# A two-block network: a convolution without GpSimd, and a state space preparation with own work tiles, lagged matmuls and loads one tile ahead

## The chip, the cores and the metric

The kernel runs on one core of one Trainium2 chip. The metric is the device time of one execution in microseconds, from the first to the last instruction of the program.

## The reference, cut to what matters

Two blocks run one after the other on 256 latent tokens and 256 context tokens of width 1024. The first block has four half-weight feed-forward layers, a convolution module and a neighbourhood attention. The second has four feed-forward layers, an attention mixer and a state space mixer (S5). The change touches the convolution, and the preparation of the state space tables from the weights alone.

```python
CONV_WIDTH = 31
def _conv_module(h, w1, b1, wdw, bdw, lng, lnb, w2, b2):
    a, gt = jnp.split(h @ w1 + b1, 2, axis=-1)
    u = a * jax.nn.sigmoid(gt)
    u = lax.conv_general_dilated(u, wdw[:, None, :], ..., feature_group_count=u.shape[-1]) + bdw
    u = jax.nn.silu(_layernorm(u, lng, lnb))
    return u @ w2 + b2
...
def s5_discretise(lam_re, lam_im, b_re, b_im, log_step):
    dt = jnp.exp(log_step)[:, None]
    mag = jnp.exp(lam_re * dt)
    a_re, a_im = mag * jnp.cos(lam_im * dt), mag * jnp.sin(lam_im * dt)
    ...
    bb_re = f_re[..., None] * b_re - f_im[..., None] * b_im
    bb_im = f_re[..., None] * b_im + f_im[..., None] * b_re
    return a_re, a_im, bb_re, bb_im
# s5_scan: x_t = a * x_{t-1} + bb u_t ;  y_t = Re(c x_t), in both directions
```

The kernel runs the scan in blocks of eight steps. For that it needs, for each of eight tiles of state groups, the powers of `a`, the inputs `a^k bb` (table V), the outputs `a^k c` (table O), the products of the two (a Toeplitz block, K and T) and rotations over the blocks (table E). None of these depends on the tokens.

## The kernel before, in words

**Matmuls in three passes.** A float32 weight piece of 128x1024 is loaded into `raw`, rounded to `wh` by ScalarE (L180), and the rest `wl = raw - wh` is formed by VectorE or GpSimd (L185). Each product is then three matmuls (`gemm`, L212). Which engine forms `wl` is set by `self.cvm`: 0 gives all to VectorE, 2 gives every second one to GpSimd (L183). Feed-forward layers over both streams set it to 0 and set it back to 2 at their end, so the convolution before the change runs with 2.

**Order.** The program is written as one stream of matmuls. `mm` (L105) adds each matmul's estimated cost to a clock `pe_t`, and `tick` then steps background tasks whose time has come. A `Task` is a generator. After each `yield` it waits for its period of `pe_t`, or for the number that was yielded if that is more, and at least half a period. The tile framework then places the instructions of each engine by its own estimate of when they are ready, so the order on an engine can differ from the written one. Every engine runs its queue strictly in the resulting order. All DMAs are issued by SyncE (SP), also in order.

**Stages.** In the order of time: the feed-forward layer f100, the convolution, the layers f102 and f110, then attention and the rest. During the three feed-forward layers two tasks run beside the matmuls: the modulation vectors (`mods`, `jk` on VectorE, L535) and the preparation `s5_pre` with a period of 820.

**The convolution** (`conv`, L947) works on eight tiles of 128 channels, both streams side by side (128x512). For each tile: 48 matmuls `pj` (`pw1`), a gate `u` on VectorE (L969), then 31 taps. Eight taps go to GpSimd: ScalarE scales a shifted `u` into `pr` (L998) and GpSimd adds it to `a` (L999). Five go to TensorE as matmuls `ptap` with diagonal weights `dgw` (L1018). The other 18 go to VectorE, ScalarE making the first; two running sums `v` and `b` (L986, L1004) are added in L1007, then `a` (L1021), then the matmul's result (L1022). The matmuls of tile m's taps and its last additions (`rest`) come after the 48 matmuls of tile m+1, and the sums `pmean` for the layer norm (L1029) one tile later still. The last tile runs the streams apart, with 12 taps on TensorE, 7 on GpSimd and 12 on VectorE. Then the layer norm starts with eight subtractions (L1057).

**The preparation** (`s5_pre`, L1853) loops over eight tiles d. In each it loads B and C (`bc`, one buffer, L1955), forms powers `pn`, `pw` on VectorE, with the work tiles `pt` that the rotations use on GpSimd, then `bb` on GpSimd (L1947 to L1952), copies `bb` to `bbz` on ScalarE (L2003, L2004), and for both directions r: six GpSimd products for V (L2015 to L2025), eight transposes `pvt` on TensorE, copies back by ScalarE (L2033) into the same work tiles `w`, their store to `dV`, six GpSimd products for O in the tiles `w` again (L2041 to L2051), their store to `dO`, and eight matmuls `kp`. Then follow the rotations `E` on GpSimd (L2079 to L2098), also in tiles `w`, and the Toeplitz loads and stores (L1967, L1969).

## Time and profile before

| what | value |
|---|---|
| time, median of three runs | 3753.76 us |
| lowest and highest of the three | 3747.49 and 3756.62 us |
| the profiled execution | 3753.8 us |
| its span, first to last instruction | 3752.0 us |
| mean granted TensorE clock | 0.963 of full speed |
| TensorE matmul, VectorE, ScalarE, GpSimd busy | 93%, 71%, 38%, 32% |

The profile is one execution. A page and several views of its trace were read: the busy share of each engine in stretches of time, groups of instructions by line and shape with the idle time of the engine just before them and what ended it, who waited for whom, and the instructions of a stretch in order of time. PE is TensorE, DVE is VectorE, ACT is ScalarE, POOL is GpSimd and SP is SyncE. A full TensorE clock is written 1.00; half is 0.5.

### The profile page before, as it was taken

Reading aid. Unit: us, or ns where it says so; the run is one execution under the profiler, and the core shown is the slowest. Engines: PE = TensorE matmul, PEld = TensorE weight load, DVE = VectorE, ACT = ScalarE, POOL = GpSimd, SP = SyncE. Lnnn points to the kernel's source line nnn. Section 1 sums busy time; section 2 is a strip of 40 time slices with the busy share of each in tenths; the row PEclk is TensorE's granted clock in tenths of the full one; section 3 lists DMA queues with packets and bytes.
Section 4 is the critical chain, followed back from the end, with each engine's and each line's share of the span. In section 5 each row is a group of like instructions: output and inputs, shape, how many; then the busy total and the mean of one; then the engine's idle time right before and its main releaser. Section 6 shows DMA issues by size and latency. Waiting matters only on the chain. (4 is left out here: it accounts for less than half of the span.)

```text
span 3752.0 us, 54881 instructions
## 1 busy us (share of the span) xinstructions
PE 3495.2 (93%) x21110; PEld 3055.5 (81%) x21110; DVE 2652.6 (71%) x4326; ACT 1424.2 (38%) x2500; POOL 1218.5 (32%) x1057
## 2 busy tenths in 40 slices
PE   8989977999999899998999998999999999997898
PEld 7767855988898687898998888778888988885798
DVE  7988699776669786777987775786665633368633
ACT  4222344532233223555343223565322432243443
POOL 5545366244445355213430003333000300035343
PEclk9999988999999999999999999999999999998899
DMA  7565310254546863424655542103555332238353
GB/s 258 184 207 194 118 57 34 102 192 164 167 146 211 293 211 130 144 89 160 244 217 199 185 165 96 62 29 107 180 192 178 135 124 92 100 114 281 113 191 125
DMA packets 158127, 580.42 MB, mean 155 GB/s; under 512 B 25252, under 2 KB 56740, under 8 KB 118184
## 3 DMA queue, kind: packets, MB, share of 16 engines
q1 hardware_dynamic: 157864, 576.91, 44.4%
q8 instruction: 166, 2.72, 0.3%
q14 instruction: 97, 0.79, 0.1%
HBM read 547.55 MB, written 29.29 MB: 154 GB/s over the span
## 5 line engine op out<-in xcount | busy, mean ns | idle before, releaser
L180 ACT ACTIVATE wh<-raw 128x1024 fp32r<-128x1024 f32 (+1 forms) x679 | 701.2, 1038 | 1268.4 <-PE gu L106 728.5
L106 PE MATMUL gu<-hl,wh 128*128 128x512 f32 (+1 forms) x3136 | 1084.6, 347 | 5.4 <-DVE hl L693 4.4
L106 PE MATMUL gu<-hh,wh 128*128 128x512 f32 (+1 forms) x3136 | 1078.9, 348 | 8.4 <-ACT hh L690 7.8
L106 PE MATMUL gu<-hh,wl 128*128 128x512 f32 (+1 forms) x3136 | 1083.2, 347 | 2.8 <-DVE wl L185 2.5
L185 DVE TENSOR_TENSOR wl<-raw,wh 128x1024 fp32r<-128x1024 f32 (+1 forms) x537 | 694.1, 1295 | 401.2 <-ACT wh L180 389.8
L185 POOL TENSOR_TENSOR wl<-raw,wh 128x1024 fp32r<-128x1024 f32 (+1 forms) x142 | 360.1, 2537 | 1259.4 <-ACT wh L180 1214.7
L535 DVE CUSTOM_DVE_ANT_0 jk<-mw,cb,vec 128x1024 bf16<-128x1024 f32 x480 | 705.8, 1470 | 29.7 <-DMA mw<-in_mw_dram 19.0
L106 PEld LDWEIGHTS gu<-hl,wh 128*128 128x128 f32 x3136 | 600.5, 192 | 79.1 <-DVE hl L693 6.1
L106 PEld LDWEIGHTS gu<-hh,wh 128*128 128x128 f32 x3136 | 597.0, 192 | 81.7 <-ACT hh L690 9.4
L106 PEld LDWEIGHTS gu<-hh,wl 128*128 128x128 f32 x3136 | 600.2, 192 | 74.3 <-DVE wl L185 3.5
L106 PE MATMUL pd<-Hh,wh 128*128 128x256 f32 (+1 forms) x1696 | 562.7, 334 | 27.4 <-ACT Hh L779 27.3
L106 PE MATMUL pd<-Hl,wh 128*128 128x256 f32 (+1 forms) x1696 | 563.6, 334 | 1.6 <-DVE Hl L780 1.5
L106 PE MATMUL pd<-Hh,wl 128*128 128x256 f32 (+1 forms) x1696 | 563.5, 334 | 0.0
L106 PEld LDWEIGHTS pd<-Hh,wh 128*128 128x128 f32 x1696 | 323.9, 192 | 60.3 <-ACT Hh L779 29.3
L106 PEld LDWEIGHTS pd<-Hl,wh 128*128 128x128 f32 x1696 | 324.5, 192 | 33.5 <-DVE Hl L780 2.8
L106 PEld LDWEIGHTS pd<-Hh,wl 128*128 128x128 f32 x1696 | 324.5, 192 | 30.3 <-issue 0.2
L777 DVE TENSOR_TENSOR gu<-sg,gu 128x512 f32<-128x512 f32 (+1 forms) x196 | 113.2, 578 | 205.5 <-PE gu L106 196.0
L106 PE MATMUL pj<-hh,wh 128*128 128x256 f32 (+1 forms) x736 | 230.4, 330 | 16.9 <-ACT hh L690 6.9
L106 PE MATMUL pj<-hh,wl 128*128 128x256 f32 (+1 forms) x736 | 232.3, 320 | 0.9 <-DVE wl L185 0.9
L106 PE MATMUL pj<-hl,wh 128*128 128x256 f32 (+1 forms) x736 | 231.1, 319 | 1.7 <-DVE hl L1086 1.0
L779 ACT ACTIVATE Hh<-gu 128x512 fp32r<-128x512 f32 (+1 forms) x196 | 98.7, 503 | 287.6 <-DVE gu L777 287.6
L106 PEld LDWEIGHTS pj<-hh,wh 128*128 128x128 f32 x736 | 145.5, 206 | 28.9 <-ACT hh L690 8.2
(407 smaller groups left out, 4656.3 us busy)
## 6 DMA issues: line engine op xcount, KB each, us to landing
raw<-in_gu_dram SPq DMA_DIRECT2D x186, 1024.0 KB, 4.8
mw<-in_mw_dram SPq DMA_DIRECT2D x280, 512.0 KB, 4.2
raw<-in_dn2b_dram SPq DMA_DIRECT2D x38, 1024.0 KB, 4.7
raw<-in_dn1b_dram SPq DMA_DIRECT2D x32, 1024.0 KB, 6.2
raw<-in_dn1a_dram SPq DMA_DIRECT2D x16, 768.0 KB, 4.3
raw<-in_pw_dram SPq DMA_DIRECT2D x12, 1024.0 KB, 4.7
raw<-in_dn2a_dram SPq DMA_DIRECT2D x16, 768.0 KB, 4.2
dV<-w SPq DMA_DIRECT2D x32, 256.0 KB, 4.2
```

Source lines behind the costliest of these rows:

```text
L106: ins = self.last_mm = self.nc.tensor.matmul(out=out, lhsT=lhsT, rhs=rhs, start=start, stop=stop, **kw)
L180: ins = nc.scalar.activation(out=h2, in_=r, func=AF.Copy)
L185: self.low_p = lambda eng=eng, l2=l2, r=r, h2=h2: eng.tensor_sub(l2, r, h2.bitcast(F32))
L535: self.behind_pe(nc.vector.tensor_tensor_reduce(out=jk, in0=tl[i], in1=self.cb[s], scale=1.0, scalar=self.V(f"mod_b{b}{l}")[:, j:j + 1], o ...
L777: nc.vector.tensor_mul(pr[:, :n], sg[:, :n], pu[:, :n])
L779: nc.scalar.activation(out=hi, in_=pr[:, :n], func=AF.Copy)
```

## The change

In the convolution GpSimd gets no taps. TensorE takes 8 instead of 5 (14 instead of 12 on the last tile), and VectorE and ScalarE the remaining 23, of which ScalarE makes the first of each running sum, so VectorE has 21 instead of 16 scaled additions. The addition of `a` (L1021) and the scaled copies for it (L987, L998) are gone. All `wl` of the convolution go to VectorE (`cvm = 0`).

In the preparation the period becomes 1500. `bc` and `pw` get two buffers, and `bc` of tile d+1 is loaded at the start of tile d. VectorE's powers use their own work tiles `pq`. The V products have tiles `vw`, the O products `ow` and the transposed V `vt`. The copies to `bbz` move from ScalarE to GpSimd. The steps stand in another order: V and O products of direction 1, then the transposes of V; V of direction 0, then the `kp` matmuls of direction 1; and so on, so that each matmul is written some steps after the product that it reads.

```diff
-    def conv(self, ready, gate, after, NPE=5, NPOOL=8, L=1, n1_=12, n2_=7):
+    def conv(self, ready, gate, after, NPE=8, L=1, n_last=14):
...
-                pk, ek, dk = range(n_pool), range(n_pool, n_pool + n_pe), list(range(n_pool + n_pe, W))
+                ek, dk = range(n_pe), list(range(n_pe, W))
...
-                first = [nc.vector.tensor_scalar(b2, src(dk[1]), w(dk[1]), None, ALU.mult)]
-                nc.scalar.activation(out=a2, in_=src(0), func=AF.Copy, scale=w(0))
+                nc.scalar.activation(out=b2, in_=src(dk[1]), func=AF.Copy, scale=w(dk[1]))
+                first = []
...
-                for k in pk[1:]:
-                    diagonal()
-                    pr = cp.tile([128, 2, T], F32, tag="pr", name="pr", bufs=2)[:, :ns]
-                    nc.scalar.activation(out=pr, in_=src(k), func=AF.Copy, scale=w(k))
-                    nc.gpsimd.tensor_add(a2, a2, pr)
...
-                    nc.vector.tensor_add(vm, vm, a2)
                     nc.vector.tensor_add(vm, vm, pe)
...
+            self.cvm = 0
             w0 = [self.take() for _ in range(2)]
...
-            bc = sp.tile([128, 4, 2, 4, 16], F32, tag="bc", name="bc")
+            bc = sp.tile([128, 4, 2, 4, 16], F32, tag="bc", name="bc", bufs=2)
...
+        ahead = load(0)
         for d in range(8):
-            bc = load(d)
+            bc = ahead
+            if d < 7:
+                ahead = load(d + 1)
...
-                a.activation(out=bbz[i][0:64, :, :, 0:16], in_=bb[i][0:64], func=AF.Copy)
-                a.activation(out=bbz[i][64:128, :, :, 16:32], in_=bb[i][64:128], func=AF.Copy)
+                g.tensor_copy(bbz[i][0:64, :, :, 0:16], bb[i][0:64])
+                g.tensor_copy(bbz[i][64:128, :, :, 16:32], bb[i][64:128])
...
-                A, B, C = [sp.tile([128, 4, 9, 16], F32, tag=f"w{i}", name=f"w{i}") for i in range(3)]
+                A, B, C = [sp.tile([128, 4, 8, 16], F32, tag=f"vw{i}", name=f"vw{i}") for i in range(3)]
...
-                    vt = (C8, A8)[i].rearrange("p q e h -> p (q e h)")
+                    vt = sp.tile([128, 512], F32, tag=f"vt{i}", name=f"vt{i}")
...
-                A, B, C = [sp.tile([128, 4, 9, 16], F32, tag=f"w{i}", name=f"w{i}") for i in range(3)]
+                A, B, C = [sp.tile([128, 4, 9, 16], F32, tag=f"ow{i}", name=f"ow{i}") for i in range(3)]
...
+            V1 = yield from inputs(1)
+            O1 = yield from outputs(1)
+            yield from turned(1, V1)
+            V0 = yield from inputs(0, lambda: store_outputs(1, O1))
+            yield from steps(1, O1)
+            O0 = yield from outputs(0)
+            yield from turned(0, V0)
+            E = yield from rotations()
+            store_outputs(0, O0)
+            yield from steps(0, O0)
+            store_rotations(E)
...
-            pre = Task(self, self.s5_pre(sp), 820)
+            pre = Task(self, self.s5_pre(sp), PRE_STEP)
```

`turned` holds the transposes `pvt`, `steps` the matmuls `kp`, `inputs` and `outputs` the six GpSimd products each. The scratch for dynamic DMA descriptors is also cut to 1024, which gives room in the on-chip memory.

How the instructions now stand is shown at three places. The first is VectorE in the convolution, around the end of one tile's taps. `u` is the gated input of a tile, `v` and `b` its running sums, `a` GpSimd's sum. Before:

```order
L969 SCALAR_TENSOR_TENSOR u_3858<-th,t 128x256 x2
L1004 SCALAR_TENSOR_TENSOR v_3869<-u_3857,vec,v_3869 128x512
L1004 SCALAR_TENSOR_TENSOR b_4570<-u_3857,vec,b_4570 128x512
L986 TENSOR_SCALAR b_4703<-u_3858,vec 128x512
L1004 SCALAR_TENSOR_TENSOR v_3870<-u_3858,vec,v_3870 128x512
L1007 TENSOR_TENSOR v_3869<-v_3869,b_4570 128x512
L1004 SCALAR_TENSOR_TENSOR b_4703<-u_3858,vec,b_4703 128x512
...
L1021 TENSOR_TENSOR v_3869<-v_3869,a_4569 128x512
...
L1022 TENSOR_TENSOR v_3869<-v_3869,ptap 128x512
```

And VectorE at the end of a tile's taps in the changed kernel, with its own line and buffer numbers:

```order
L186 TENSOR_TENSOR wl<-raw,wh 128x1024
L995 SCALAR_TENSOR_TENSOR b_4442<-u_3892,vec,b_4442 128x512
...
L998 TENSOR_TENSOR v_3903<-v_3903,b_4319 128x512
L970 SCALAR_TENSOR_TENSOR u_3893<-th,t 128x256 x2
L995 SCALAR_TENSOR_TENSOR v_3904<-u_3892,vec,v_3904 128x512
...
L1012 TENSOR_TENSOR v_3903<-v_3903,ptap 128x512
...
L995 SCALAR_TENSOR_TENSOR v_3905<-u_3893,vec,v_3905 128x512
```

The addition of `a` and the first scaling of `b` are gone from VectorE, and from tile to tile there are two `wl` where there was one; the taps of neighbouring tiles interleave as before.

The second place is ScalarE in f100, at the start of the preparation's second tile. `Hh` and `sg` belong to the feed-forward layer, `wh` to its weights. Before:

```order
L779 ACTIVATE Hh_701<-gu 128x512
L2003 ACTIVATE bbz_1013<-bb_2211 64x8x16
L2004 ACTIVATE bbz_1013<-bb_2211 64x8x16
L180 ACTIVATE wh<-raw 128x1024
L775 ACTIVATE sg<-gu 128x512
L2003 ACTIVATE bbz_1014<-bb_2212 64x8x16
L2004 ACTIVATE bbz_1014<-bb_2212 64x8x16
...
L779 ACTIVATE Hh_702<-gu 128x512
```

ScalarE at the same place in the changed kernel:

```order
L780 ACTIVATE Hh_701<-gu 128x512
L181 ACTIVATE wh<-raw 128x1024
L776 ACTIVATE sg<-gu 128x512
...
L780 ACTIVATE Hh_702<-gu 128x512
L181 ACTIVATE wh<-raw 128x1024 x5
L2037 ACTIVATE vt_2522<-pvt 128x512
```

The four copies to `bbz`, which read what GpSimd makes from the loaded `bc`, no longer stand ahead of the feed-forward layer's own work.

The third place is GpSimd in the first tile of the preparation, at the end of V's products for direction 1. Before:

```order
L2019 TENSOR_TENSOR w_1168<-w_1168,w_1170 128x512
L2023 TENSOR_TENSOR w_1170<-pw_1022,bb_1099 128x512
L2025 TENSOR_TENSOR w_1169<-w_1169,w_1170 128x512
L2047 TENSOR_TENSOR w_1360<-pw_1022,bc 128x576
L2043 TENSOR_TENSOR w_1361<-pw_1022,bc 128x576
L2041 TENSOR_TENSOR w_1359<-pw_1021,bc 128x576
L2045 TENSOR_TENSOR w_1359<-w_1359,w_1361 128x576
```

GpSimd at the same place in the changed kernel:

```order
L2009 TENSOR_TENSOR vw_1327<-pw_1180,bb_1287 128x512
L2017 TENSOR_TENSOR vw_1328<-pw_1180,bb_1288 128x512
L2046 TENSOR_TENSOR ow_1404<-pw_1180,bc 128x576
L2011 TENSOR_TENSOR vw_1329<-pw_1181,bb_1288 128x512
L2048 TENSOR_TENSOR ow_1406<-pw_1181,bc 128x576
L2052 TENSOR_TENSOR ow_1405<-pw_1181,bc 128x576
L2013 TENSOR_TENSOR vw_1327<-vw_1327,vw_1329 128x512
```

Before, the O products write the buffers that the V store still reads; now both kinds have their own tiles and interleave.

## Rows read from the trace of the kernel before

**Rows 1.** The page, part 1: busy us, share of span, instructions of each engine.

```profile
PE 3495.2 (93%) x21110; PEld 3055.5 (81%) x21110; DVE 2652.6 (71%) x4326; ACT 1424.2 (38%) x2500; POOL 1218.5 (32%) x1057
```

**Rows 2.** Stretches: busy us and instructions per engine, clock, DMA share, GB/s.

```profile
250.00:300.00 50.00, 39.34 (x183) 32.01 (x184) 46.67 (x63) 13.32 (x18) 28.10 (x20) 0.86 0.58 191
...
550.00:600.00 50.00, 32.78 (x113) 22.92 (x113) 50.00 (x52) 23.11 (x43) 30.29 (x17) 0.85 0.13 42
...
950.00:1000.00 50.00, 50.00 (x239) 40.99 (x238) 30.84 (x37) 15.46 (x22) 27.07 (x18) 1.00 0.44 150
...
1250.00:1300.00 50.00, 36.57 (x166) 29.13 (x165) 45.26 (x55) 14.23 (x22) 28.37 (x19) 0.88 0.85 299
```

**Rows 3.** DVE groups, 470 to 650 us: count, busy us, mean ns, idle before.

```profile
L1004 DVE SCALAR_TENSOR_TENSOR v<-u,vec,v 128x512 f32<-128x512 f32 x56 | 69.7, 1251 | 0.0
L1004 DVE SCALAR_TENSOR_TENSOR b<-u,vec,b 128x512 f32<-128x512 f32 x56 | 65.1, 1169 | 0.1
L185 DVE TENSOR_TENSOR wl<-raw,wh 128x1024 fp32r<-128x1024 f32 x7 | 11.7, 1666 | 6.1 <-ACT wh L180 6.1
...
L1021 DVE TENSOR_TENSOR v<-v,a 128x512 f32<-128x512 f32 x7 | 8.0, 1141 | 0.0
```

**Rows 4.** DVE in order of time: start us, us, instruction, count; idle before.

```profile
541.01 3.46 DVE L1004 SCALAR_TENSOR_TENSOR v<-u,vec,v 128x512 f32<-128x512 f32 x2
544.39 3.43 DVE L1004 SCALAR_TENSOR_TENSOR b<-u,vec,b 128x512 f32<-128x512 f32 x2
...
556.82 0.74 DVE L1004 SCALAR_TENSOR_TENSOR v<-u,vec,v 128x512 f32<-128x512 f32 x1
557.49 0.74 DVE L1004 SCALAR_TENSOR_TENSOR b<-u,vec,b 128x512 f32<-128x512 f32 x1
...
644.63 2.74 DVE L1057 TENSOR_TENSOR v<-v,pmean 128x256 f32<-128x256 f32 x8 [1.52 <-PE pmean L106]
```

**Rows 5.** POOL in order of time, the same stretch of the convolution.

```profile
540.86 11.47 POOL L999 TENSOR_TENSOR a<-a,pr 128x512 f32<-128x512 f32 x7 [3.92 <-ACT pr L998]
```

**Rows 6.** PE in order of time, 538 to 562 us.

```profile
542.66 0.39 PE L106 MATMUL pj<-hh,wl 128*128 128x512 f32 x1
542.89 4.46 PE L106 MATMUL ptap<-u,dgw 128*128 128x512 f32 x10
...
547.41 0.39 PE L106 MATMUL pj<-hl,wh 128*128 128x512 f32 x1
...
558.88 2.07 PE L106 MATMUL pmean<-v,invm 128*128 128x256 f32 x4 [9.00 <-DVE v L1022]
```

**Rows 7.** Line L1004: ns shortest/median/longest, first and last start us, shapes.

```profile
L1004 DVE SCALAR_TENSOR_TENSOR b<-u,vec,b x66: 472/743/2898, 472.8 to 656.5; 128x512 f32<-128x512 f32 x56, 128x256 f32<-128x256 f32 x10
```

**Rows 8.** PE groups of the whole span: busy us, mean ns, idle before them.

```profile
L106 PE MATMUL pd<-Hh,wh 128*128 128x512 f32 x768 | 299.8, 392 | 19.7 <-ACT Hh L779 19.7
...
L106 PE MATMUL pvt<-cst,w 128*128 128x128 f32 x128 | 19.5, 277 | 6.3 <-POOL w L2019 4.5 <-POOL w L2025 1.8
...
L106 PE MATMUL kp<-w,bbz 128*32 128x128 f32 x256 | 14.7, 297 | 24.0 <-POOL w L2051 14.0 <-POOL w L2045 10.0
...
L106 PE MATMUL pmean<-v,invm 128*128 128x256 f32 x32 | 11.8, 503 | 27.7 <-DVE v L1022 27.7
```

**Rows 9.** Four engines in order of time around one stall of f100.

```profile
249.53 0.40 POOL L1947 TENSOR_TENSOR pt<-bc,cfr 128x128 f32<-128x128 f32 x1 [29.10 <-DMA bc<-in_s5bc_dram]
...
250.85 0.31 ACT L2003 ACTIVATE bbz<-bb 64x128 f32<-64x128 f32 x1 [9.23 <-POOL bb L1949]
...
259.30 0.68 DVE L777 TENSOR_TENSOR gu<-sg,gu 128x512 f32<-128x512 f32 x1
...
260.66 0.80 PE L106 MATMUL pd<-Hh,wh 128*128 128x512 f32 x1 [14.79 <-ACT Hh L779]
```

**Rows 10.** POOL's waits over the span: us in total, times, longest us.

```profile
POOL w L2043 <- DMA dV<-w: 177.5, 16, 18.0
POOL pt L1947 <- DMA bc<-in_s5bc_dram: 135.8, 5, 31.6
```

More of the change, by code (lines that the diff above doesn't have):

```diff
@@ L973, in conv, with taps @@
             tail_, last_ = [None], [None]
-            def taps(m, ss, n_pe=NPE, n_pool=NPOOL):
+            def taps(m, ss, n_pe=NPE):
                 s0, ns = ss[0], len(ss)
@@ L1125, in conv @@
                         layernorm(LAT)
-                    taps(m, [s], *((n1_, n2_) if m == KT - 1 else ()))
+                    taps(m, [s], *((n_last,) if m == KT - 1 else ()))
             self.release(2 * L)
@@ L1977, in s5_pre @@
             pn = [sp.tile([128, 8, 9], F32, tag=f"pn{i}", name=f"pn{i}") for i in range(2)]
-            pw = [sp.tile([128, 2, 4, 9], F32, tag=f"pw{i}", name=f"pw{i}") for i in range(2)]
+            pw = [sp.tile([128, 2, 4, 9], F32, tag=f"pw{i}", name=f"pw{i}", bufs=2) for i in range(2)]
             pt = [sp.tile([128, 8, 32], F32, tag=f"e{i}", name=f"pt{i}") for i in range(2)]
+            pv = [sp.tile([128, 8, 4], F32, tag=f"pq{i}", name=f"pq{i}") for i in range(2)]
             v.memset(pn[0][:, :, 0:1], 1.0)
@@ L2051, in s5_pre, with store_outputs @@
                 g.tensor_sub(B, B, C)
-                yield 6000
+                yield
+                return A, B
+            def store_outputs(r, AB):
                 k0 = 1 - r
-                for i, s_ in enumerate((A, B)):
+                for i, s_ in enumerate(AB):
                     nc.sync.dma_start(
@@ L2057, in s5_pre, with steps @@
                         in_=s_[:, :, k0:k0 + 8, :].rearrange("p q e h -> p q (e h)"))
+            def steps(r, AB):
+                A, B = AB
                 kp = self.psa.tile([128, 512], F32, tag="a", name="kp")
[L2060 removed]
                 x0, x1, o0 = (1, 9, 0) if r == 1 else (0, 8, 112)
@@ L2073, in s5_pre @@
                     v.tensor_add(kt[:, 112:128], kt[:, 112:128], kp[:, 112:128])
-                yield 3000
-            nc.sync.dma_start(out=self.dK[d], in_=kt)
-            E = [sp.tile([128, 8, 72], F32, tag=f"w{i}", name=f"E{i}") for i in range(2)]
-            E = [e.rearrange("p a b -> p (a b)")[:, :512].rearrange("p (a b) -> p a b", a=8) for e in E]
-            g.memset(E[0][:, :, 0:1], 1.0)
-            g.memset(E[1][:, :, 0:1], 0.0)
-            for i, t in enumerate((c8, s8)):
-                g.tensor_copy(E[i].rearrange("p (d q) e -> p d q e", d=2)[:, :, :, 1], col(t))
@@ L2101, in s5_pre, with rotations @@
-            yield 5000
-            for r in range(2):
-                for i, t in enumerate(E):
-                    nc.sync.dma_start(out=self.dE[d][r][:, i * 256:i * 256 + 256],
-                                      in_=t[:, 4 * r:4 * r + 4, :].rearrange("p q e -> p (q e)"))
-                yield
+                yield
+            def rotations():
+                E = [sp.tile([128, 8, 64], F32, tag=f"vw{i}", name=f"E{i}") for i in range(2)]
+                g.memset(E[0][:, :, 0:1], 1.0)
+                g.memset(E[1][:, :, 0:1], 0.0)
+                for i, t in enumerate((c8, s8)):
+                    g.tensor_copy(E[i].rearrange("p (d q) e -> p d q e", d=2)[:, :, :, 1], col(t))
+                yield
+                k = 1
+                while k < 63:
+                    n = min(k, 63 - k)
+                    X = [p[:, :, 1:1 + n] for p in E]
+                    Y = [p[:, :, k:k + 1].to_broadcast([128, 8, n]) for p in E]
+                    O = [p[:, :, k + 1:k + 1 + n] for p in E]
+                    t1, t2 = pt[0][:, :, :n], pt[1][:, :, :n]
+                    g.tensor_mul(t1, X[0], Y[0])
+                    g.tensor_mul(t2, X[1], Y[1])
+                    g.tensor_sub(O[0], t1, t2)
+                    if n > 4:
+                        yield
+                    g.tensor_mul(t1, X[0], Y[1])
+                    g.tensor_mul(t2, X[1], Y[0])
+                    g.tensor_add(O[1], t1, t2)
+                    k += n
+                    yield
+                return E
@@ new lines, in store_rotations @@
+            def store_rotations(E):
+                for r in range(2):
+                    for i, t in enumerate(E):
+                        nc.sync.dma_start(out=self.dE[d][r][:, i * 256:i * 256 + 256],
+                                          in_=t[:, 4 * r:4 * r + 4, :].rearrange("p q e -> p (q e)"))
+            V1 = yield from inputs(1)
[3 more added lines that the diff above has]
+            yield from steps(1, O1)
```

81 lines of the change are left out of this document (33 added, 48 removed).

## The prediction

> **What bounds the kernel now.** I read the page's busy shares first: TensorE is busy 93% of the span [rows 1], so the time is the matmul stream plus the stretches in which it stands still or runs at half clock. Next the stretches [rows 2], to find where those are. Around 950 us, in f102, TensorE is busy 50.00 of 50 us at clock 1.00, although the preparation's GpSimd steps run beside it. Around 250 us (f100) and 1250 us (f110) it has 39.34 and 36.57 of 50 us, and around 550 us, in the convolution, 32.78. So there are two places with something to gain, and they have different limits.
>
> In the convolution VectorE is the limit: 50.00 of 50 us [rows 2]. Its groups [rows 3] show why it takes so long: the full-width scaled additions have a mean of about 1.2 us. In order of time [rows 4] one takes 0.74 us and the next starts 0.67 us later when GpSimd is still, at 556.82 and 557.49. From 541.01 two take 3.38 us until the next pair starts, 1.69 us each, and in the same stretch GpSimd makes seven additions in 11.47 us, 1.64 us each [rows 5]. The two engines take turns: an addition of one waits for an addition of the other. TensorE waits for the result: `pmean` was idle 27.7 us for VectorE's last addition, 9.00 of them at 558.88 [rows 6, 8].
>
> In f100 and f110 it is the preparation that stops TensorE. At 249.53 GpSimd's first product of a tile had waited 29.10 us for the load of `bc`. ScalarE, whose copy to `bbz` stood next in its queue, waited 9.23 us for that, and behind it stood the feed-forward layer's own `wh`, `sg` and `Hh`. VectorE's `gu` came at 259.30 and TensorE stood still for 14.79 us [rows 9]. The groups of TensorE [rows 8] add the waits that the transposes `pvt` (6.3 us) and the matmuls `kp` (24.0 us) make for GpSimd. GpSimd itself was late because it waited for stores and loads: 177.5 us for `dV`, whose source shares its tiles, and 135.8 us for `bc` [rows 10].
>
> **The change part by part: the convolution.** I follow VectorE from its first tap at 472.8 us [rows 7] to the end of the eight subtractions that open the layer norm, 644.63 + 2.74 = 647.4 us [rows 4]: 174.6 us now. Afterwards GpSimd does nothing in the loop, so VectorE's operations have their price alone. One full tile:
> - 21 scaled additions at 0.67 us: 14.1 us.
> - Two sums, `v + b` and `v + ptap`, at the same 0.67 us: 1.3 us.
> - Two gates of half width. The shortest scaled addition, a half-width one, lasts 0.47 us and the full one 0.74 [rows 7], so a half-width one starts about 0.40 us after the other: 0.8 us.
> - Two `wl` instead of one. With GpSimd beside it one took 1.67 us [rows 3], the upper end. It has twice the columns of a 0.67 us addition and one fixed part, so I take 1.2 us, an estimate: 2.4 us.
>
> That is 18.6 us for a tile, 130 us for seven. The last tile's first stream has 15 half-width additions, two sums and a gate, 18 x 0.40 = 7.2 us, and the subtractions take 2.7 us as now. The sum is 140 us, 34.6 us less.
>
> TensorE must keep up with that. One `pj` follows another after 0.23 us (542.66 to 542.89); five taps take from 542.89 to 547.41 less one `pj`, 4.29 us, so 0.86 us a tap [rows 6]. A tile afterwards is 48 x 0.23 + 8 x 0.86, 17.9 us, and `pmean` with four records of about 0.2 us adds 0.9: 18.8 us. Today it is 16.2 us, hidden under VectorE. So the three more taps (2.6 us a tile, 18 us in all, and 14 instead of 12 in each half of the last tile) find cover, but all of it is used: the two engines come out equal at 18.6 and 18.8 us. I give 2 us back for their waits on each other and take **33 us** off. The ends: 44 us if the price of an addition is nearer 0.66 and a `wl` nearer its share, with the engines overlapping fully; 15 us if they wait for each other a fifth of the time. ScalarE makes the first of each sum and eight diagonals instead of five, but loses eight scaled copies a tile, so it has less. The layer norm's tail after 647.4 us stays as it is, since GpSimd takes `wl` there before and after.
>
> **The preparation.** What is lost now: `pd` 19.7, `pvt` 6.3 and `kp` 24.0 us of idle TensorE [rows 8], 50.0 us. After each long stall the clock is at half for a while: the first matmul after the stall at 260.66 is 0.80 us long where the same shape has a mean of 0.39 [rows 8, 9], and the clock means of 0.86 and 0.88 in the two stretches [rows 2] are 14 and 12 us at half, most of them idle. I put 1.7 us to each of five stalls, an estimate: 8 us. Together 58 us.
>
> What takes them away: `bc` is loaded a tile ahead, so the wait of 29.10 us before a tile goes. The copies to `bbz` go to GpSimd, so ScalarE's queue holds nothing that waits for GpSimd's first product. 32 copies at 0.31 us [rows 9] are 10 us more on GpSimd, covered by 177.5 + 135.8 = 313 us that it no longer waits [rows 10]; without that cover they would delay the tile's first transposes by 1.2 us. V and O products have their own tiles, so the 177.5 us for `dV` go. Each `pvt` and `kp` is written six to twelve GpSimd steps after its product. At up to 1.5 us of matmul time a step that is 9 to 18 us, where six products at the 1.64 us of a contended addition [rows 5] need 9.8 us.
>
> Of the queues that are passed: on SP the load of `bc` stands at the start of the tile before and finds a free buffer, so nothing behind it (weight and modulation loads) waits for it. The `dO` stores move to a place where their source has been written for some steps. On TensorE nothing is added; two transposed halves now hold two of the three buffers that the norms' sums use too, worth at most some 2 us at each of three stage ends. VectorE's powers no longer share work tiles with GpSimd's rotations.
>
> What is late next in f100 and f110 is VectorE, with 46.67 and 45.26 of 50 us [rows 2]; f102, where it has 30.84, shows no loss with the same GpSimd steps. I leave 10 us of the 58 to waits for VectorE and take **48 us** off. Ends: 58 and 20.
>
> The profiled execution took 3753.8 us, the same as the median of the runs. 3753.8 - 33 - 48 = **3673 us**. Everything behind both places hangs on the matmul stream, so nothing gives it back later.
>
> **The rivals.**
> - *The convolution stays coupled.* `v + ptap` stands on VectorE between the next tile's additions, and both engines need 18.7 us, so a wait on one side is passed to the other. If most of the 27.7 us before `pmean` [rows 8] remains, the convolution gives 12 us: 3753.8 - 12 - 48 = 3694 us. Against it: the gates of a tile stand where TensorE still has a tile of `pj` to do. Chance 0.12.
> - *GpSimd is late again.* VectorE in f100 and f110 still reads two on-chip operands beside it, so its products keep their contended price, and the first transposes of a tile wait as now. Only the `bbz` stall goes, and the preparation gives 10 us: 3711 us. Against it: the 313 us of waits [rows 10] are 39 us a tile. Chance 0.10.
> - *Slower: late at every group.* There are 16 groups of `pvt` and 16 of `kp`. If the shorter way from products to matmuls makes each wait w, and each brings 1.7 us of half clock, the loss is 32 (w + 1.7) us against 58 now. It outweighs the convolution's 33 us from w = 1.15 us on; with w = 2 us the time is 3753.8 - 33 + 118 - 58 = 3781 us. For it: a tile's twelve products at 1.64 us are 19.7 us, more than twelve steps of 1.5. Chance 0.04.
> - *The additions keep their price.* If the 1.2 us [rows 3] were VectorE's own, a tile would be 21 x 1.2 + 1.3 + 0.8 + 2 x 1.67 = 30.6 us against 174.6 / 7 = 24.9 now: the convolution grows by 40 us, 3753.8 + 40 - 48 = 3746 us. Against it: 0.67 us at 556.82 [rows 4]. Chance 0.03. The Trainium skill ("Perfetto Trace Analysis", Optimizing Scalar/DVE Operations) says that with a saturated VectorE it may make sense to move work to ScalarE or even GpSimd, which is the opposite of this change; the same place warns that those two share a read port, so that moving work between them might not help. By the first half the convolution would lengthen like this; the trace bears out the second, with 1.69 us beside GpSimd and 0.67 us without.
>
> **How the numbers follow.** A measurement of this kernel tells about 0.3%, 11 us, from no change. The forecast has 0.71, the rivals 0.12, 0.10, 0.04 and 0.03. Faster by over 0.3% are the forecast and the first two rivals, 0.93. Within 0.3% is the last, 0.03. Slower is 0.04. The forecast's own ends are 3753.8 - 44 - 58 = 3652 and 3753.8 - 15 - 20 = 3719 us. The range for 8 in 10 runs from 3645, a little below the first, as the half-clock share is an estimate, to 3710 us, which takes in the first rival and ends at the second.
>
> **What would show it.** Right: in the convolution no full-width scaled addition longer than 0.75 us, tiles 18 to 20 us apart, the subtractions ending some 33 us earlier after the first tap than now, and the TensorE clock near 1.00 there. In f100 and f110, `kp`, `pvt` and `pd` together with under 15 us of idle time, no wait of GpSimd for `dV` or `bc`, no `bbz` on ScalarE. Wrong: `pmean` or `ptap` still idle for over 20 us; `gu` or `pd` waiting for VectorE in f100 because it has become the limit there; long waits of TensorE for the products `vw` or `ow`.

## The result, and the profile after

The changed kernel takes 3697.76 us, the median of 4 runs (3695.96 to 3699.76), beside 3750.62 us for the kernel before (4 runs, 3745.89 to 3756.62): a ratio of 0.9851, 95% interval 0.9839 to 0.9864. That is 53 us faster. I had forecast 81 us, 3673 us as the time, and 3645 to 3710 us as the range.

The table takes each stage from the start of its first matmul to that of the next stage, starts read to 0.1 us, in the two profiled executions. Their spans, 3752.0 and 3694.2 us, are 57.8 us apart; the medians of the runs 53.

| stage | before, us | after, us | gain | forecast |
|---|---|---|---|---|
| f100 | 416.8 | 411.5 | 5.3 | } 48 |
| f102 and f110 | 791.8 | 781.6 | 10.2 | } together |
| convolution | 269.9 | 230.9 | 39.0 | 33 |
| everything behind | 2244.2 | 2241.0 | 3.2 | 0 |

The convolution did a little more than forecast, the preparation a third of it. "Everything behind" is not touched by the change, and over all kernels of this document it lies between 2236.5 and 2244.3 us, so its 3.2 us are no effect of it. The changed kernel's busy shares answer [rows 1]:

```profile
PE 3493.0 (95%) x21160; PEld 3053.7 (83%) x21160; DVE 2644.1 (72%) x4360; ACT 1383.1 (37%) x2430; POOL 1193.0 (32%) x1021
```

The stretches of [rows 2], and two more of f100 (columns as there: length, then PE, PEld, DVE, ACT, POOL busy, clock, DMA share, GB/s):

```profile
150.00:200.00 50.00, 47.97 (x229) 38.73 (x228) 49.97 (x86) 10.94 (x17) 41.38 (x42) 1.00 0.57 188
200.00:250.00 50.00, 40.72 (x186) 31.68 (x184) 49.76 (x82) 11.70 (x17) 44.40 (x37) 0.99 0.57 181
250.00:300.00 50.00, 41.00 (x170) 33.27 (x171) 44.85 (x68) 10.26 (x12) 12.89 (x7) 0.88 0.67 239
550.00:600.00 50.00, 48.91 (x231) 36.55 (x229) 48.50 (x81) 14.56 (x31) 0.00 (x0) 1.00 0.08 30
950.00:1000.00 50.00, 50.00 (x223) 41.40 (x222) 30.57 (x31) 14.75 (x19) 26.34 (x21) 1.00 0.56 192
1250.00:1300.00 50.00, 41.84 (x165) 33.22 (x164) 43.87 (x59) 13.89 (x17) 13.07 (x7) 0.86 0.74 259
```

At 550 us TensorE went from 32.78 to 48.91 of 50 us and the clock from 0.85 to 1.00: the convolution is cured. At 250 and 1250 us TensorE still stands still: 41.00 and 41.84 of 50 us, clock 0.88 and 0.86. (The row at 1250 us shows work that came some 44 us later in the kernel before.) From 150 to 250 us VectorE is now busy without a pause, and GpSimd 41 to 44 of 50 us beside it.

The convolution in more detail: VectorE in order of time (start, us, instruction, count), then all its scaled additions (shortest, median, longest in ns, first and last start), then the subtractions. They answer [rows 4, 7].

```profile
532.52 0.68 DVE L1012 TENSOR_TENSOR v<-v,ptap 128x512 f32<-128x512 f32 x1
...
540.36 1.41 DVE L995 SCALAR_TENSOR_TENSOR b<-u,vec,b 128x512 f32<-128x512 f32 x2
541.69 1.41 DVE L995 SCALAR_TENSOR_TENSOR v<-u,vec,v 128x512 f32<-128x512 f32 x2
...
551.20 0.68 DVE L1012 TENSOR_TENSOR v<-v,ptap 128x512 f32<-128x512 f32 x1
```

```profile
L995 DVE SCALAR_TENSOR_TENSOR v<-u,vec,v x93: 472/743/2566, 467.9 to 615.5; 128x512 f32<-128x512 f32 x77, 128x256 f32<-128x256 f32 x16
```

```profile
L1047 DVE TENSOR_TENSOR v<-v,pmean x8: 410/412/420, 602.3 to 604.6; 128x256 f32<-128x256 f32 x8
```

Two additions take 1.33 us from start to start, 0.67 each, against 1.69 at [rows 4]. In the middle one tile follows the other after 18.7 us (532.52 to 551.20). The way from first tap to last subtraction is 467.9 to 605.0, 137.1 us, where I had worked out 140.

TensorE's groups over the whole span answer [rows 8] (count, busy us, mean ns, idle before them and what ended it):

```profile
L107 PE MATMUL pd<-Hh,wh 128*128 128x512 f32 x768 | 302.4, 396 | 21.9 <-ACT Hh L780 20.2 <-DVE Hl L781 1.7
L107 PE MATMUL pd<-Hl,wh 128*128 128x512 f32 x768 | 302.2, 394 | 3.9 <-DVE Hl L781 3.9
...
L107 PE MATMUL pvt<-cst,vw 128*128 128x128 f32 x128 | 19.8, 277 | 8.2 <-POOL vw L2013 7.1 <-POOL vw L2021 1.1
...
L107 PE MATMUL kp<-ow,bbz 128*32 128x128 f32 x256 | 11.7, 279 | 0.0
L107 PE MATMUL pmean<-v,invm 128*128 128x256 f32 x32 | 8.6, 391 | 3.5 <-DVE v L1012 3.5
```

`pmean` fell from 27.7 to 3.5 us and `kp` from 24.0 to nothing. `pvt` stayed (6.3 to 8.2) and so did `pd` (19.7 to 21.9). For the three of the preparation that is 50.0 against 30.1 us, 19.9 us less; 3.6 us more before `Hl` come off again, and the 16.3 us left are close to the 15.5 us of the table.

What the `pd` stalls of f100 now wait for: four engines around one of them, in order of time. They answer [rows 9].

```profile
243.09 2.43 DVE L536 CUSTOM_DVE_ANT_0 jk<-mw,cb,vec 128x1024 bf16<-128x1024 f32 x1
...
245.57 1.95 DVE L536 CUSTOM_DVE_ANT_0 jk<-mw,cb,vec 128x1024 bf16<-128x1024 f32 x1
...
247.46 0.69 DVE L778 TENSOR_TENSOR gu<-sg,gu 128x512 f32<-128x512 f32 x1
```

```profile
242.05 2.40 POOL L2050 TENSOR_TENSOR ow<-ow,ow 128x576 f32<-128x576 f32 x1
244.41 2.04 POOL L2011 TENSOR_TENSOR vw<-pw,bb 128x512 f32<-128x512 f32 x1
246.40 2.14 POOL L2054 TENSOR_TENSOR ow<-pw,bc 128x576 f32<-128x576 f32 x1
```

```profile
248.17 0.60 ACT L780 ACTIVATE Hh<-gu 128x512 fp32r<-128x512 f32 x1 [9.57 <-DVE gu L778]
```

```profile
248.83 0.79 PE L107 MATMUL pd<-Hh,wh 128*128 128x512 f32 x1 [4.96 <-ACT Hh L780]
```

ScalarE no longer has a `bbz` in its queue; it waits 9.57 us for VectorE's `gu`. VectorE is not waiting for anything: ahead of `gu` stand its reductions `jk` for the modulations and a `wl`, and each takes 1.9 to 2.4 us, while GpSimd's products run back to back beside them.

The stall in f110, in the stretch from 1250 us, is of another kind:

```profile
1264.36 1.06 ACT L507 ACTIVATE cb<-cb 128x1024 f32<-128x1024 f32 x1 [6.24 <-DMA cb<-in_c_dram]
1266.90 0.79 PE L107 MATMUL pd<-Hh,wh 128*128 128x512 f32 x1 [3.30 <-ACT Hh L780]
1268.40 1.27 DVE L536 CUSTOM_DVE_ANT_0 jk<-mw,cb,vec 128x1024 bf16<-128x1024 f32 x1
1287.58 1.80 POOL L2009 TENSOR_TENSOR vw<-pw,bb 128x512 f32<-128x512 f32 x1 [34.55 <-PE pvt L107]
```

GpSimd does nothing from 1253 to 1287.58 us, and `jk` takes 1.27 us. Here `cb`, the input of the next modulation vectors, stands in ScalarE's queue and waits 6.24 us for its load, with `Hh` behind it. `pd` waits 3.30 us for that, and 4.02 more at 1277.30, when VectorE makes up its late `jk`. So two thirds of the `pd` waits lie in f100, most of them with GpSimd's products beside VectorE (the longest, 6.37 us at 262.23, also holds 2.81 us in which VectorE waits for a load of `mw`). The last third lies in f110, behind a load at the head of ScalarE's queue.

GpSimd's waits answer [rows 10] (us in total, times, longest):

```profile
POOL vw L2009 <- PE pvt L107: 215.0, 7, 36.5
```

The waits for `dV` and `bc`, 313 us at [rows 10] and 37.8 us more for `dV` at line L2041, are gone, but GpSimd waits 215.0 us at the start of a tile for the `pvt` of the tile before, that is, for the pace at which the steps are written.

### The profile page after: what moved, and what is told of

Read it like the earlier page. It is cut to its first block, busy times and chain, and to the rows that moved or that the text cites. A ratio compares the mean times of both kernels' runs of the same rounds, so it can differ in the third digit from the quotient of the medians.

```text
span 3694.2 us, 54763 instructions
## 1 busy us (share of the span) xinstructions
PE 3493.0 (95%) x21160; PEld 3053.7 (83%) x21160; DVE 2644.1 (72%) x4360; ACT 1383.1 (37%) x2430; POOL 1193.0 (32%) x1021
## 5 line engine op out<-in xcount | busy, mean ns | idle before, releaser
L186 DVE TENSOR_TENSOR wl<-raw,wh 128x1024 fp32r<-128x1024 f32 (+1 forms) x544 | 706.6, 1300 | 366.4 <-ACT wh L181 358.7
L186 POOL TENSOR_TENSOR wl<-raw,wh 128x1024 fp32r<-128x1024 f32 (+1 forms) x135 | 342.2, 2537 | 1283.5 <-ACT wh L181 1245.6
```

The costliest lines, as they stand in the source:

```text
L186: self.low_p = lambda eng=eng, l2=l2, r=r, h2=h2: eng.tensor_sub(l2, r, h2.bitcast(F32))
```

## The experiments

Stages are measured as in the table above. Ratios are to the kernel before, run beside each of them.

**The two parts apart (e1, e2).** The first kernel has the hunks of `conv` alone, the second those of the preparation alone.

```diff
# the convolution alone (label e1), among others
-                    nc.gpsimd.tensor_add(a2, a2, pr)
...
-                    nc.vector.tensor_add(vm, vm, a2)
...
# the preparation alone (label e2), among others
-            bc = load(d)
+            bc = ahead
...
-                a.activation(out=bbz[i][0:64, :, :, 0:16], in_=bb[i][0:64], func=AF.Copy)
+                g.tensor_copy(bbz[i][0:64, :, :, 0:16], bb[i][0:64])
...
```

> The kernel before with the convolution's edits alone (all taps' additions on VectorE, sums of 23 taps by one vm += b2, the lagged TensorE taps), preparation as before. Theory C (my prediction's: GpSimd's two-input additions were what stretched VectorE's additions beside them): the convolution from its first matmul to the third feed-forward's first falls from 269.9 us to about 231 as in the changed kernel, everything else stays, 3750.6 - 39 = about 3712 us. Rival (part of the convolution's gain in the changed kernel came from the preparation's part, which lets VectorE enter the convolution with less behind it, or the other way round): the gain differs from 39 by more than 8 us.

> The changed kernel with the old convolution, so the preparation's edits alone. If the parts add up: first feed-forward -5, the two later ones -10, about 3735 us (-16). If my forecast of the preparation (-48) held by itself and only the new convolution takes some of it away: 3703 us. Either way the idle time of TensorE before pvt, kp and pd together tells: about 35 us (parts add up) or under 15.

Measured: 3713.16 us (0.9881, 0.9864 to 0.9897) and 3737.13 us (0.9947, 0.9932 to 0.9962). In e1 the convolution takes 230.3 us and f100 416.5; in e2 the convolution takes 270.2 us, f100 411.6, f102 and f110 780.1. Each part does in its own stages what it does in the whole. The two ratios take off 1.2% and 0.5%, the whole 1.5%, so within their intervals the parts add up. One stage moved that its edit does not touch: in e1 f102 and f110 take 797.7 us, 6 more than before, and why is not known. The preparation by itself is no better than in the changed kernel (`pd`, `pvt` and `kp` are idle for 30.2 us in e2, as the first case has it), so the new convolution takes nothing from it.

**The convolution: GpSimd's additions put back, with nobody waiting for them (e6).** The three tiles `dm` are set to zero once.

```diff
+            dm = [cp.tile([128, 2, T], F32, name=f"dm{i}") for i in range(3)]
...
                 ek, dk = range(n_pe), list(range(n_pe, W))
+                if ns == 2:
+                    for k in dk[:7]:
+                        nc.gpsimd.tensor_add(dm[k % 2], src(k), dm[2])
```

> The changed kernel with 7 additions of 128x512 on GpSimd for each of the convolution's 8 tiles, reading the tile's taps' input and a constant, and read by nobody: no engine waits for their results. Theory C (taking turns is what the old convolution paid): beside them VectorE's additions take 1.2 us and more instead of 0.67, the tile grows from 18.8 to about 24 us, the convolution from 230.9 to about 275 us, total about 3740. Rival (the old convolution paid for VectorE's and TensorE's waits for GpSimd's results, not for the turns): the convolution stays within 8 us of 230.9.

Measured: 3738.06 us (0.9953, 0.9936 to 0.9969), convolution 270.0 us. The groups of VectorE and of GpSimd from 470 to 645 us:

```profile
L1001 DVE SCALAR_TENSOR_TENSOR v<-u,vec,v 128x512 f32<-128x512 f32 x76 | 75.7, 1026 | 0.0
L1001 DVE SCALAR_TENSOR_TENSOR b<-u,vec,b 128x512 f32<-128x512 f32 x70 | 68.9, 1009 | 0.0
```

```profile
L987 POOL TENSOR_TENSOR dm<-u,dm 128x512 f32<-128x512 f32 x47 | 75.3, 1634 | 69.4 <-DVE u L973 69.4
```

The additions' mean is 1.02 us (0.74 in the changed kernel), tiles follow each other after 24.0 us in the middle (18.5 to 25.6 over all), and the convolution takes 270.0 us again instead of 230.9, although no engine waits for a result of GpSimd. So turns alone cost this kernel 39 us: theory C holds, and the rival, waits for results, is not needed. The edit covers the seven tiles with both streams side by side, 49 additions, not eight tiles as the expectation says. That 270.0 us are also the time of the kernel before is partly chance: VectorE had 16 scaled additions a tile there (112 for seven tiles, [rows 3]) instead of 21, one `wl` instead of two, and was just as late. It won nothing by giving GpSimd a part of the additions.

**The preparation: is it the powers that moved forward (e4)?** In the changed kernel the scheduler puts 90 of the powers' multiplications and additions ahead of the convolution on VectorE; before it was 54. The trace has 144 of them in all, where the expectation says 208.

```diff
-            pw = [sp.tile([128, 2, 4, 9], F32, tag=f"pw{i}", name=f"pw{i}", bufs=2) for i in range(2)]
+            pw = [sp.tile([128, 2, 4, 9], F32, tag=f"pw{i}", name=f"pw{i}") for i in range(2)]
...
-            pv = [sp.tile([128, 8, 4], F32, tag=f"pq{i}", name=f"pq{i}") for i in range(2)]
+            pv = pt
```

> The changed kernel with pw back at one buffer and the powers' scratch back in the tiles of pt, so that the powers of a tile can't run ahead: 54 of their 208 multiplications and additions stand ahead of the convolution on VectorE instead of 90, pw 12 instead of 16. Theory H (the powers that were moved forward into the first feed-forward, some 36 x 0.30 us and more, are what loads VectorE there): first feed-forward 411.5 -> about 399 us, TensorE's waits for Hh and Hl there fall by more than half, total about 3687. Theory T (GpSimd's two-input products beside it, now without pauses, take turns with VectorE): the first feed-forward stays within 4 us of 411.5, the total within 6 us of 3697.8, and jk beside GpSimd still takes 2 us and more.

Measured: 3693.85 us (0.9832, 0.9818 to 0.9847), f100 409.6 us, f102 and f110 784.0. The changed kernel, run once more with other runs (e7), gave 3697.15 us:

> The changed kernel once more, beside the next three on one chip: 0.985 of the kernel before, as at first.

Its ratio was 0.9841, 0.9824 to 0.9857. The intervals of the two lie over each other, so by the middle values the powers cost some 3 to 7 us, and perhaps nothing. Judged by the time, theory H falls: as theory T wants it, f100 is 1.9 us shorter only. But TensorE's waits for `Hh` and `Hl` in f100 did fall, from 20.6 to 11.4 us, nearly by the half that theory H wanted; `pvt` took up part of it, waiting 6.0 us for products there instead of 1.1.

**GpSimd's reads taken away (e3).** On top of that edit, every product, sum and difference of `inputs` and `outputs` writes a constant:

```diff
-                g.tensor_mul(A, pr, br)
+                g.memset(A, 0.5)
...
-                g.tensor_add(A, A, C)
+                g.memset(A, 0.5)
...
```

> As the run with the old power tiles, but the 24 products, sums and differences of inputs and outputs of each of the 8 tiles on GpSimd are replaced by writes of a constant to the same tiles (the values of the state space matrices are left out, so that part of the output is not computed); waits, copies, matmuls, DMAs and rotations stay. Compare it with the run with the old power tiles. Theory T (GpSimd's reads take VectorE's turns): VectorE's busy time in the first feed-forward falls by 25 us or more, TensorE no longer waits for Hh or Hl there, first feed-forward shorter by 10 to 20 us, the two later ones by another 10 to 20, total 20 to 40 us less. Theory H (VectorE's own added work): under 8 us less.

Measured: 3666.63 us (0.976, 0.9745 to 0.9774), 27 us less than its base. f100 takes 386.5 us instead of 409.6, f102 and f110 775.3 instead of 784.0. VectorE's two dearest groups from 30 to 384 us, first with the products, then without:

```profile
L536 DVE CUSTOM_DVE_ANT_0 jk<-mw,cb,vec 128x1024 bf16<-128x1024 f32 x108 | 164.1, 1519 | 0.8
L186 DVE TENSOR_TENSOR wl<-raw,wh 128x1024 fp32r<-128x1024 f32 x51 | 73.8, 1448 | 3.1 <-ACT wh L181 2.2 <-DMA cls<-in_s5ls_dram 0.8
```

```profile
L536 DVE CUSTOM_DVE_ANT_0 jk<-mw,cb,vec 128x1024 bf16<-128x1024 f32 x112 | 144.6, 1291 | 3.7 <-DMA mw<-in_mw_dram 2.9
L186 DVE TENSOR_TENSOR wl<-raw,wh 128x1024 fp32r<-128x1024 f32 x56 | 69.3, 1238 | 5.8 <-ACT wh L181 5.0
```

The same instructions are 0.23 and 0.21 us shorter each. VectorE's busy time over f100, with the products and without:

```profile
30.00:439.00 409.00, 390.58 (x1889) 324.93 (x1889) 357.72 (x589) 118.56 (x176) 266.36 (x221) 0.97 0.58 197
```

```profile
30.00:417.00 387.00, 383.52 (x1892) 321.08 (x1893) 314.50 (x589) 119.12 (x176) 156.17 (x209) 1.00 0.61 207
```

Both have 589 instructions of VectorE. So 43 us of its 357.7 were turns. With them gone the stage takes 386.5 us, at clock 1.00. Theory T holds for f100; for f102 and f110 I had put 10 to 20 us, and it was 9, and there TensorE still waits 6.7 us for `Hh`, after ScalarE has waited 7.4 us for a load of `cb`. The 23 us of f100 can be split: about 10 us are waits for `Hh` and `Hl` (11.4 to 1.0 us), 6.0 are the waits of `pvt` for products, and 7 are TensorE's busy time, which fell with the clock back at 1.00. The run also makes GpSimd quicker (0.52 us for what took 2), so the 32 us of both stages bound the cost of the turns from above; the shorter `jk` and `wl` are the turns themselves.

**Copies with one input in their place (e11)**, on the changed kernel:

```diff
-                g.tensor_mul(A, pr, br)
+                g.tensor_copy(A, pr)
...
```

> The changed kernel with the 24 products, sums and differences of inputs and outputs of each tile replaced by copies of their first input to the same tile on GpSimd (the values of the state space matrices are left out, so that part of the output is not computed). If any read of GpSimd takes turns with VectorE: jk in the first feed-forward stays above 1.45 us on average and the first feed-forward above 405 us. If only its two-input operations do: jk falls to about 1.29 us and the first feed-forward to about 388 us, as with the products replaced by writes of a constant; total about 3667.

Measured: 3667.58 us (0.976, 0.9744 to 0.9777), f100 390.2 us. The total is as expected of the second case, but its reason is wrong: copies take turns too. `jk` in f100 takes 1.36 us on average, between the two cases, against 1.49 in the changed kernel. GpSimd in order of time, beside a `wl` of VectorE from 130.86 and a `jk` that takes 1.63 us from 132.00:

```profile
130.29 0.61 POOL L2009 COPY vw<-pw 128x512 f32<-128x512 f32 x1 [3.00 <-DVE pw L1989]
130.85 1.70 POOL L2017 COPY vw<-pw 128x512 f32<-128x512 f32 x1
132.50 1.66 POOL L2046 COPY ow<-pw 128x576 f32<-128x576 f32 x1
134.10 0.61 POOL L2013 COPY vw<-vw 128x512 f32<-128x512 f32 x1
```

A copy takes 0.61 us without a `jk` or `wl` beside it and 1.66 to 1.70 with one. That it hurts less because it is short fits the longest `jk` in f100, 1.76 us, 0.48 more than by itself, where products made it up to 1.17 more; GpSimd is also sooner through, and the run does not part the two.

A constant written by GpSimd took 0.52 us (e3, 128x512) and left `jk` nearly at its own time. The Trainium skill ("SBUF — State Buffer", Who interferes with whom) states this rule: a VectorE instruction with two inputs in SBUF contends with a GpSimd instruction that reads SBUF, and not with one that only writes it. The runs agree on both halves: 1.52 us with reads and 1.29 us with writes.

**The steps spread otherwise (e5, e8).** If VectorE loses its time where GpSimd's products run beside the modulations, it should help to move tiles from f100, where modulations are dense, to f102, where VectorE has 30.84 of 50 us to do [rows 2]. The period between two steps is set for each stage (f100, f102, f110):

```diff
# one tile in f100, 4 in f102, 3 in f110
-            pre = Task(self, self.s5_pre(sp), PRE_STEP)
+            pre = Task(self, self.s5_pre(sp), 3000)
...
             self.mark("f102")
+            pre.period = 800
...
             self.mark("f110")
+            pre.period = 1500
```

The first run has none in f100 (no `side` there, then 700 and 1200), the second the diff above, both with the old power tiles (e5); the third is the changed kernel with this diff alone (e8).

> The run with the old power tiles, and the preparation not stepped in the first feed-forward at all: its 8 tiles are stepped at a period of 700 in the third feed-forward (4 tiles instead of 3) and of 1200 in the next one (4 instead of 3). Theory T (VectorE is the limit of the first feed-forward, by the preparation's own work and by GpSimd's reads beside it): the first feed-forward falls from 409.6 to about 386 us, as with GpSimd's products left out; the two later ones take on what two tiles need there. In the third feed-forward VectorE is busy 262 of 388 us, so its share costs little; the next one has VectorE at 315 of 390 and pays 5 to 15 us more waits. Total 3675 to 3685. Rival (GpSimd at 84 us a tile is the limit when 4 tiles are put into 388 us): TensorE waits for vw and for the sums of outputs again, 20 us or more, and the total is 3695 or above.

> As the run before, but with one tile in the first feed-forward (period 3000), 4 in the third (period 800) and 3 in the next (1500). Theory T: first feed-forward about 398 us, half way between 386 and 409.6, the fourth tile in the third feed-forward costs under 5 us, the next one as with the old power tiles; total about 3683. Rival (what counts is only how many tiles the first feed-forward carries beyond the point where VectorE is full): first feed-forward 388 or less.

> The changed kernel, its power tiles as they are, with the steps alone spread otherwise: period 3000 in the first feed-forward (1 tile of 8 instead of 2), 800 in the third (4 instead of 3), 1500 in the next (3). If the spread alone gave the 30 us (VectorE's overfull first feed-forward is the cause, the own power tiles are not): first feed-forward about 384 us, total within 6 us of 3667. If the old power tiles are needed for it: first feed-forward 395 or more, total 3680 or more.

| tiles in f100, f102, f110 | f100, us | f102 and f110, us | total, us | ratio, 95% interval |
|---|---|---|---|---|
| 2, 3, 3 (old power tiles, above) | 409.6 | 784.0 | 3693.85 | 0.9832, 0.9818 to 0.9847 |
| 0, 4, 4 | 376.2 | 818.4 | 3697.24 | 0.9842, 0.9827 to 0.9857 |
| 1, 4, 3 | 381.5 | 785.0 | 3667.29 | 0.9764, 0.9749 to 0.9778 |
| 1, 4, 3, own power tiles | 383.9 | 783.1 | 3669.93 | 0.9765, 0.9751 to 0.978 |

With one tile in f100, 28 us are won there and nothing is given back. These two kernels beat both others, and the changed one by 27 to 30 us. The spread alone does it, as e8 has the changed kernel's own tiles. My middle value for one tile in f100, 398 us, was wrong: the cost is not in proportion to the tiles, the second one pays nearly all of it. With none in f100 the rival came true: `pvt` waited 21.9 us for products, GpSimd was busy 312.55 of 390 us from 640 us on, and all of f100's gain was lost. That load alone is not the limit: with one tile in f100 GpSimd was busy 298.81 of the same 390 us, at a period of 800 instead of 700, and `pvt` did not wait.

f100 in the changed kernel and in e8:

```profile
30.00:441.00 411.00, 388.12 (x1890) 322.06 (x1889) 369.67 (x631) 117.85 (x177) 263.84 (x223) 0.98 0.58 196
```

```profile
30.00:413.00 383.00, 379.31 (x1831) 318.22 (x1831) 341.94 (x603) 114.58 (x168) 174.98 (x142) 1.00 0.57 198
```

VectorE's busy share is the same, 90% and 89%, with 20 us of TensorE's waits in the one and 2.7 us in the other. Its share does not tell whether it is the limit. What differs is GpSimd: 263.84 against 174.98 us. I read it so that VectorE's work in f100 is mostly `jk`, which is not urgent by itself and fills any gap; a `gu` comes late when the `jk` and `wl` that the order puts ahead of it take 2 us and more each, for as long as a run of products lasts. That the length of such a run decides, and not the sum, is argued, not shown.

A last try slowed the steps in f102 and f110 (e10, 900 and 1800 instead of 800 and 1500):

> As the run with one tile in the first feed-forward and the old power tiles, but a period of 900 instead of 800 in the third feed-forward and 1800 instead of 1500 in the next one, where VectorE is busy 327 of 400 us and TensorE waits 8.5 us for Hh and Hl. If those waits come from the preparation's work falling into the same 50 us as the modulations': 3 to 8 us less there, total about 3662. If they come from the modulations alone: within 3 us of 3667.

Measured: 3676.81 us (0.978, 0.9765 to 0.9794), f102 and f110 794.1 instead of 785.0. I expected a gain or nothing. From f100 to f110 `pd` waited for `Hh` 20.3 us, against 7.5 in the faster run: the products of a tile now ran from 1200 us on (GpSimd 37.26 of 50 us, before 24.81), and TensorE had 36.50 of 50 us there. The first of the two long stalls, 8.33 us, stands behind a wait of 8.59 us for the load of `cb`; the second, 8.07 us at 1258.2, beside products and `jk` of 2.2 us. Dense products alone are not enough for a stall: from 1200 to 1250 us the changed kernel has GpSimd busy 47.91 of 50 us and TensorE 50.00. So where a run of products falls seems to matter more than the pace, which is argued from these few stretches. How to place them well in f110 stays open.

**The loads (e9).** On the changed kernel, each tile loads its own `bc` again:

```diff
-            bc = sp.tile([128, 4, 2, 4, 16], F32, tag="bc", name="bc", bufs=2)
+            bc = sp.tile([128, 4, 2, 4, 16], F32, tag="bc", name="bc")
...
-        ahead = load(0)
         for d in range(8):
-            bc = ahead
-            if d < 7:
-                ahead = load(d + 1)
+            bc = load(d)
```

> The changed kernel with bc back at one buffer and each tile's loads issued as the tile begins. If the loads ahead carry a large part of the preparation's gain (they were the largest single wait at 250 us in the kernel before): TensorE's waits for pd and kp rise, 10 us or more of the 16 go. If not (GpSimd's late start of a tile is now covered by the work that waits for VectorE): within 5 us of the changed kernel.

Measured: 3700.83 us (0.9849, 0.9834 to 0.9864), so the same as the changed kernel beside it. GpSimd's waits:

```profile
POOL pt L1939 <- DMA bc<-in_s5bc_dram: 236.9, 7, 46.5
```

GpSimd waits 236.9 us for loads, more than before the change, and the end does not move by more than 4 us. It took the place of the 215.0 us that it waits for `pvt`. The run leaves the copies to `bbz` on GpSimd, so it prices the loads ahead alone; no run puts those copies back on ScalarE.

## Why the prediction was right and wrong

- **The total lies in the range of 3645 to 3710 us, in part by luck.** The preparation gave a third of what I had put, outside its own ends; 6 us more from the convolution, 3 from stages that the change does not touch, and a range wide enough for the first rival kept the time inside.
- **The convolution, 33 us off, ends 44 and 15: right, with its mechanism.** 39.0 us. A tile was to take 18.6 us on VectorE and 18.8 on TensorE; it takes 18.7. VectorE's sum was 140 us and is 137.1. No full-width addition takes over 0.76 us; the longest of all, two of half width with 2.57 us, stand beside two `wl` of GpSimd. The 2 us that I gave back for waits of the two engines were not needed: the rival that they stay coupled is out, with `pmean` at 3.5 us. The rival of the additions' own price is out by those 0.76 us and by e6.
- **The preparation, 48 us off, ends 58 and 20: wrong**, with 15.5 us, and this is the whole miss (32 us, of which the convolution and what lies behind it gave 9 back). The step that failed is the last one, "I leave 10 us of the 58 to waits for VectorE". `pd`, `pvt` and `kp` together were to be idle for under 15 us; it is 34.0 with the waits for `Hl`. The idle time before `pd` was to be nearly all gone; it is 25.8 us for `Hh` and `Hl`, and the stretches with half clock stayed with it: f100 has a mean clock of 0.98 before and after.
- Of the three terms, `kp` was right: 24.0 us to nothing, as written six to twelve steps later. `pvt`, 6.3 us, stayed at 8.2; I gave six products 9.8 us of the steps' 9 to 18; at the 2.0 to 2.4 us that they take beside a busy VectorE they need 12 to 14. `bbz` was mis-sized too: I gave a copy 0.31 us, and on GpSimd the first copy of a pair takes 1.23 us in the median. `pd` was read rightly for the kernel before, where `bbz` stood in front of `Hh`, and wrongly for what follows. That wait and the `bbz` copies are gone, and other stalls have come in their place; with the wait for `bc` put back (e9) the time is the same.

**Why VectorE was sized wrongly.** A stretch of f100 in the kernel before, and the whole stage; the rows of after for both stand above.

```profile
200.00:250.00 50.00, 45.78 (x201) 37.26 (x199) 35.64 (x78) 9.66 (x13) 19.33 (x33) 1.00 0.65 213
30.00:446.00 416.00, 388.77 (x1888) 322.83 (x1888) 348.31 (x587) 123.26 (x188) 223.13 (x203) 0.98 0.57 193
```

I had named it as what is late next, and the sign "`gu` or `pd` waiting for VectorE in f100" came true. But I took its load from the kernel before, 46.67 of 50 us, as if it were fixed. It depends on GpSimd: in this stretch GpSimd was busy 19.33 us before, and VectorE 35.64; after it is 44.40 and 49.76. The change removed the pauses and brought the products closer together. The turns as such are not new: `jk` takes 1.49 us on average in f100 before and after, and with nearly the same number of instructions VectorE is busy 348.31 us in the kernel before, 357.72 in e4 and 314.50 in e3. Of the 43 us that e3 takes away, some 34 were there already, and TensorE stood still for other things. I applied the price of taking turns to the convolution and to GpSimd's products, and not to VectorE's `jk` and `wl` beside them, though the prediction itself says that both read two on-chip operands.

e3 sizes it: 43 us of VectorE's time in f100, 23 us of the stage, and 9 us of f102 and f110. That this makes the missing 32 is no proof, since it is a bound from above. In f102 and f110 the miss has another part: TensorE's waits for GpSimd's products fell from 22.8 to 7.1 us there, and those for `Hh` and `Hl` rose from 1.2 to 8.2, behind the load of `cb` and not beside GpSimd. The prediction's own mechanism, a queue held by a load, was at work there a second time, and I had not foreseen it.

The rivals and the rest:

- The rival "GpSimd is late again" had nearly the right price for the preparation, 10 us, and its premise came true: the products keep their contended price, and `pvt` waits as before. But most of what is late is VectorE, and the `kp` waits that it keeps are gone. The slower rival, late at every group, did not happen: 8.2 us over 32 groups. In the last rival, "those two" are VectorE and GpSimd.
- What I took from f102, that it shows no loss with the same steps, was right and worth more than I made of it: it was the place for the work (e5, e8).

## What to carry to other kernels

Before you free an engine from its waits, ask what its instructions cost the engine beside it, and what else stands in the queues behind the wait: here two thirds of the gain expected from it did not come. A wait that ended last is worth only what lies between it and the next one; put it back in the new kernel to see (loads ahead: nothing). In this kernel GpSimd's work that reads on-chip memory did best beside a stage in which VectorE had room (e8), and its pace is worth setting stage by stage.

## What the runs showed of the hardware that I had not expected

- A reduction `jk` of 128x1024 on VectorE, in f100 of the changed kernel, takes 1.28 us in the 30 cases with no GpSimd instruction beside it, and 1.76 us on average, 2.45 at most, in the 32 that lie wholly beside GpSimd's two-input instructions.
- Both engines pay. GpSimd's products of 128x512 take 2.04 us beside `jk`, and a sum of 128x576 2.40 us. Additions on GpSimd can slow VectorE by more than they would cost it: e6's 49 lengthened the convolution by 39 us, where 49 at 0.67 us on VectorE itself would be 33, an estimate.
- GpSimd's copies with one input are lengthened as well, from 0.61 to 1.70 us, and its writes of a constant, 0.52 us (0.53 at most), are not; the 22 `jk` of f100 that lie wholly beside GpSimd in e3 take 1.29 us on average, nearly as by themselves.
